# A hybrid encoder on one core: earlier tap loads, a moved gate block and moved table loads in the second mixer, a second buffer for blocks of b in the first

## The chip, the cores and the metric

The kernel runs on one core of a Trainium2 chip. The metric is the device time of one execution in microseconds (us); less is better. Several executions are timed and their median is given. Beside them stands one profiled execution, with a trace of every instruction on the five engines: PE (TensorE, matrix products; PEld are its weight loads), DVE (VectorE), ACT (ScalarE), POOL (GpSimd) and SP (SyncE, which only issues transfers here). ACT and POOL issue transfers as well.

## The reference

Two layers work on 256 tokens of 1024 features. Each has a mixer (a gated convolution beside a bidirectional state-space branch, "S5") and a feed-forward part, dense in layer 0 and with eight experts in layer 1. The change touches the mixers alone. Cut to what they compute:

```python
h = rms_norm(x, norm_mix_g[layer])
z = h @ w_in[layer]                       # 1024 -> 3584
conv_v, conv_g, ssm_u, gate_conv, gate_ssm = jnp.split(z, split_at, axis=-1)

# convolution branch: 512 channels, 31 taps, one filter per channel
c = conv_v * sigmoid(conv_g)
c = depthwise_conv(c, dw_w) + dw_b
br_conv = silu(layer_norm(c, ln_g, ln_b)) @ w_conv_proj

# S5 branch: 32 groups of 16 channels, 64 complex states, both directions
s[t] = a * s[t-1] + (q * b) @ u[t]        # a, q from a_re, a_im, log_dt
y[t] = Re(c @ s[t]) (both directions) + d * u[t]
y = gelu(y); y = y * sigmoid(y @ w_glu + b_glu)
br_ssm = y @ w_ssm_proj

x = x + (sigmoid(gate_conv) * br_conv + sigmoid(gate_ssm) * br_ssm) @ w_out
x = x + FFN(rms_norm(x, norm_ffn_g[layer]))   # dense, or top 2 of 8 experts
```

## The kernel before

Features lie on the 128 partitions and the 256 tokens along the free dimension. The program goes through the first mixer (to about 212 us), the dense feed-forward (to about 440 us), the second mixer (to about 660 us) and the experts.

**The mixer.** `z()` computes one block of 2 x 128 output columns of `w_in`, from two weight units of 512 KB each, into one PSUM tile `acc`. The blocks come in this order: two for the S5 input, four for the convolution's value and gate (`glu`), and eight gate blocks (`z_gate()`, numbered 0 to 7). Between blocks `step()` lets side work go on: the S5 scan (`sc_p`, `sc_q`, `eb`), the layer norm of the convolution (`conv_norm`), and what was put off (`later`). In layer 0 (`plain`) the weights go into PE as fp32 as they come. In layer 1 each unit is first split by ACT (`wh`) and DVE (`wl`), three units ahead at most.

**The convolution.** When half of the gated channels (`hc`) are ready, `shifted()` writes them to DRAM (one POOL transfer) and reads them back as eight shifted copies (`hs`, eight POOL transfers). `conv(h)` then does two tiles (`conv_tile`, 32 products each), and each tile needs one block of taps `dg` of 512 KB. The taps have two buffers. Each tile loads its own, on POOL's queue, behind the `hs` transfers of its half. The order in the mixer is: gate block 0, `conv(0)`, gate block 1, `conv(1)`, four more gate blocks, the S5 output for q = 0 and 1, gate block 6, q = 2 and 3, gate block 7.

**The S5 tables.** S5's output (`ssm_out`, four parts q) multiplies the states by tables `tq` and the input by a kernel `w` (w3), both made on the chip. Layer 0 makes its tables inside the mixer: DVE computes `tq`, and `build_g(q)` multiplies it on PE by a block of b (`bd`, 256 KB), and writes the result to DRAM (`gd`, half of it from POOL, half from ACT), from where w3 is read back by POOL. `bd` has one buffer, and POOL loads it:

```python
def load_bd(self, l, q):
    self.bd = self.bdp.tile([128, 8, 2, 2, 16], F32, name="bd")
    self.nc.gpsimd.dma_start(self.bd.rearrange("p g r h c -> p (g r h c)"), self.a["bd"][l, q])
```

Layer 1's tables are made during the dense feed-forward (`park`) and parked in DRAM (`dw`, `dt`, `gd`). In the second mixer `fetch` reads a parked `dt` back as `ft`, two of 512 KB for each q, through SP's queue, and POOL reads the four w3. These twelve tiles share eight buffers, in the order w3, ft, ft for each q, so the last four tiles take over buffers that the S5 output for q = 0 and 1 has read.

**Order of the work.** PE, DVE and ACT carry out their instructions in the order in which the program writes them. POOL and SP have their transfers placed by a scheduler, and then issue them in that order: a transfer that has to wait holds up all behind it on its engine.

Of the kernel before, what the change touches and what calls it, by code (L numbers as in the profile page):

```python
# [10 lines left out]
F32 = mybir.dt.float32  # L11
# [8 lines left out]
T = 256  # L20
# [38 lines left out]
class Body:  # L59
# [181 lines left out]
    def consts(self):  # L241
        nc, cp = self.nc, self.cp
        self.par = cp.tile([128, NPAR], F32, name="par")
        nc.scalar.dma_start(self.par, self.a["par"])
        self.x = cp.tile([128, 8, T], F32, name="x")
        self.xs = self.a["xt"].rearrange("(k p) t -> p k t", p=128)
        ji = self.smallp.tile([128, 128], I32, name="ji", bufs=1)
        nc.gpsimd.iota(ji, pattern=[[1, 128]], base=0, channel_multiplier=-1)
        self.ident = cp.tile([128, 128], F32, name="ident")
        nc.vector.tensor_scalar(self.ident, ji, 0, None, op0=ALU.is_equal)  # L250
        self.ones = cp.tile([128, 1], F32, name="ones")
        nc.vector.memset(self.ones, 1.0)

        self.bgh = cp.tile([128, 8], F32, name="bgh")
        n0, k0 = COLS["bglu", 0]
        nc.vector.tensor_scalar(self.bgh, self.par[:, n0:n0 + 8], 0.5, None, op0=ALU.mult)
# [196 lines left out]
        return t, self.table_steps(t, g0, cp[0][:, 0], cp[0][:, 1], pt, ALU.subtract)  # L453

    def load_bd(self, l, q):
        self.bd = self.bdp.tile([128, 8, 2, 2, 16], F32, name="bd")
        self.nc.gpsimd.dma_start(self.bd.rearrange("p g r h c -> p (g r h c)"), self.a["bd"][l, q])

    def build_g(self, l, b, cp, gd, q, tq):

        nc = self.nc
        cp, cm = cp
        bd = self.bd
        ps = self.misc()
        for s in range(2):
            for p in range(4):
                g = 4 * s + p
                for r in range(2):
                    self.mm(ps[32 * p:32 * p + 32, s * 128:(s + 1) * 128],
                            bd[:, g, r].rearrange("p h c -> p (h c)"), tq[s][:, p, r], r == 0, r == 1)  # L470
        for s in range(2):
            for p in range(4):
                g = 4 * s + p
                for r in range(2):
                    self.mm(ps[32 * p:32 * p + 16, 256 + s * 16:256 + (s + 1) * 16],
                            b[:, r, 8 * q + g], (cp[:, 0, 8 * q + g], cm[:, 8 * q + g])[r], r == 0, r == 1)
        gsb = self.t2("gsb", [128, 9, 2, 16])
        nc.scalar.copy(gsb[:, 1:9].rearrange("p m s c -> p s m c"),
                       ps[:, :256].rearrange("p (s m c) -> p s m c", s=2, m=8))
        for p in range(4):  # L480
            nc.scalar.copy(gsb[32 * p:32 * p + 16, 0].rearrange("p s c -> p (s c)"),
                           ps[32 * p:32 * p + 16, 256:288])
        for p in range(4):
            for eng, m0, n, r0, g0 in ((nc.gpsimd, 7, 8, 0, 0), (nc.scalar, 0, 7, 16, 2)):
                eng.dma_start(gd[m0:m0 + n, :, p].rearrange("m c s d -> c m (s d)"),
                              gsb[32 * p + r0:32 * p + r0 + 16, g0:g0 + n].rearrange("c m s d -> c m (s d)"))
# [171 lines left out]
    def mixer(self, l, fed=None, after=None):  # L658
# [39 lines left out]
                pass  # L698
        else:
            dw, dt, gd, a8 = self.parked  # L700
            hh, hl, sqs = fed
            w1s = []

# [64 lines left out]
        def ssm0_out():  # L768
            yield
            pt = self.ssm_prep_out(0)  # L770
            self.ssm_q()
            yield
            cps = []
            for _ in self.ssm_cq(0, c, cps):
                pass
            cp, gd_ = cps
            tqs = []
            for h in range(9):
                if h and h % 2 == 0:
                    q = h // 2 - 1  # L780
                    self.build_g(0, b, cp, gd_[q], q, tqs[2 * q:2 * q + 2])
                    ts.append((tqs[2 * q:2 * q + 2], self.load_w3(gd_[q])))
                if h < 8:
                    t, st = self.half_t(cp, pt, 4 * h)
                    tqs.append(t)
                    if h % 2 == 0:
                        self.load_bd(0, h // 2)
                    for _ in st:
                        pass
                    yield  # L790
            k = 1
            while k < 31:
                self.ssm_scan(eb, a8, k, min(k + 4, 31))
                k += 4
                yield
            ts.append(self.ssm_states(eb))
# [72 lines left out]
                step()  # L869

        z_gate()
        conv(0)
        z_gate()
        conv(1)
        if not plain:
            for q in range(4):
                w3 = self.load_w3(gd[q], self.last_dg)
                ts.append((self.fetch(dt[q]), w3))
        sides.append(self.conv_norm(l, cv))
        for i in range(5 if plain else 4):  # L880
            z_gate()
        while len(sides):
            step()
# [102 lines left out]

    def conv_tile(self, l, c, o, hs):

        dg = self.dgp.tile([128, 4, 8, 32], F32, name="dg")
        self.last_dg = ins = self.nc.gpsimd.dma_start(dg.rearrange("p i m c -> p (i m c)"), self.a["cdg"][l, c])  # L990
        self.behind(ins.ins, self.last_hs[c // 2].ins)
        for m in range(8):
            for i in range(4):
                self.mm(o[32 * i:32 * i + 32], dg[:, i, m], hs[:, i, 4 * m:4 * m + T], m == 0, m == 7)

    def conv_bias(self, l, h, ps, cv):
        dwb = self.col("dwb", l)
# [78 lines left out]
        self.nc.gpsimd.dma_start(d, t.rearrange("p g r m -> p (g r m)"))  # L1076
        return d

    def fetch(self, ds):
        out = []  # L1080
        for d in ds:
            t = self.tb("ft", [128, 4, 2, 128])
            ins = self.nc.sync.dma_start(t.rearrange("p g r m -> p (g r m)"), d)
            self.behind(ins.ins, self.last_raw.ins)
            out.append(t)
        return out

# [73 lines left out]
    def route_feed(self):  # L1161
# [15 lines left out]
        def after(i):  # L1177
# [9 lines left out]
                products(i - 1)  # L1187
            if i == 3:
                products(3)
                self.lt = self.rp.tile([8, T], F32, name="lt")  # L1190
                nc.scalar.copy(self.lt, st[0][0:8, :T])
                self.rs = self.rms_of(st[1][:, :2])
        return after
# [530 lines left out]
    def moe_consts(self):  # L1724
# [1 line left out]
        self.iota = cp.tile([128, 128], F32, name="iota")  # L1726
        nc.gpsimd.iota(self.iota, pattern=[[1, 128]], base=0, channel_multiplier=0,
                       allow_small_or_imprecise_dtypes=True)
        io = self.smallp.tile([128, 128], I32, name="ji", bufs=1)
        nc.gpsimd.iota(io, pattern=[[1, 128]], base=0, channel_multiplier=-1)  # L1730
        self.before = cp.tile([128, 128], F32, name="before")
        nc.vector.tensor_scalar(self.before, io, 0, None, op0=ALU.is_gt)
# [109 lines left out]
    def pool(self, ctx, name, bufs, **kw):  # L1842
        if kw.get("space") != DRAM:
            kw["reuse_waits"] = "tile"
        return ctx.enter_context(self.tc.tile_pool(name=name, bufs=bufs, **kw))
# [10 lines left out]
    def run(self):  # L1856
        pool = self.pool
        with ExitStack() as ctx:
# [12 lines left out]
            with self.ordered():  # L1871
                with ExitStack() as c2:
# [2 lines left out]
                    self.setp2 = pool(c2, "set2", 1)  # L1875
                    self.hcp = pool(c2, "hc", 1)
                    self.h4p = pool(c2, "h4", 5)
                    self.bdp = pool(c2, "bd", 1)
                    self.later, self.sides, self.firsts, self.last_hs = [], [], [], [None, None]
                    self.t2p = pool(c2, "t2", 2)  # L1880
                    self.dgp = pool(c2, "dg", 2)
# [111 lines left out]
```

## Time and profile before

| | us |
|---|---|
| median of 3 runs | 1397.8 (1396.7 to 1401.72) |
| profiled execution, its own time | 1396.65 |
| span of its trace | 1394.8 |
| PE busy in the span | 1310.5 (94%) |
| DVE, ACT, POOL busy | 870.5, 622.3, 84.4 |

A span is the time from the first to the last instruction of the trace; what lies around it makes the 1.85 us between it and that execution's own time. Times in rows are us from the start of the span, unless they are marked ns. The trace gives the start, the duration and the tiles of every instruction, the idle time ahead of it, and what that idle time ended with ("<-"); "issue" stands there where the profile shows no releaser. The granted clock of PE is a share of full speed: 1.00 is 2.4 GHz and 0.50 is 1.2 GHz.

### The profile page before, as it was taken

Reading aid. Unit: us, or ns where it says so; the run is one execution under the profiler, and the core shown is the slowest. Engines: PE = TensorE matmul, PEld = TensorE weight load, DVE = VectorE, ACT = ScalarE, POOL = GpSimd, SP = SyncE. Lnnn points to the kernel's source line nnn. Section 1 sums busy time; section 2 is a strip of 40 time slices with the busy share of each in tenths; the row PEclk is TensorE's granted clock in tenths of the full one; section 3 lists DMA queues with packets and bytes.
Section 4 is the critical chain, followed back from the end, with each engine's and each line's share of the span. In section 5 each row is a group of like instructions: output and inputs, shape, how many; then the busy total and the mean of one; then the engine's idle time right before and its main releaser. Section 6 shows DMA issues by size and latency. Waiting matters only on the chain.

```text
span 1394.8 us, 23390 instructions
## 1 busy us (share of the span) xinstructions
PE 1310.5 (94%) x9324; PEld 1032.6 (74%) x9324; DVE 870.5 (62%) x1332; ACT 622.3 (45%) x905; POOL 84.4 (6%) x148
## 2 busy tenths in 40 slices
PE   7999989999998978989899999999999999999995
PEld 6877889999998967878766666666666666666663
DVE  7696676788887455774755555545555555565552
ACT  3432345444444442543445544445444545454542
POOL 1052130000121031000000000000000000000000
PEclk9999999999999999999799999999999999999996
DMA  6285535566778475544589999999999999999980
GB/s 223 87 258 163 165 126 168 174 215 209 224 236 297 143 259 173 197 137 167 204 330 421 409 421 358 364 411 420 418 398 367 421 421 420 420 401 421 421 362 32
DMA packets 78306, 399.73 MB, mean 287 GB/s; under 512 B 13024, under 2 KB 15712, under 8 KB 44400
## 3 DMA queue, kind: packets, MB, share of 16 engines
q1 hardware_dynamic: 64960, 370.70, 69.1%
q0 software_dynamic: 8448, 26.32, 5.9%
q10 hardware_dynamic: 4784, 1.16, 0.4%
q8 instruction: 75, 1.23, 0.4%
q14 instruction: 39, 0.32, 0.1%
HBM read 386.51 MB, written 11.63 MB: 285 GB/s over the span
## 4 chain that ended last, share of the span: by engine, by line
PE 59%; DVE 5%; DMA 3%; ACT 2%; issue 1%; ACTq 0%; SPq 0%; DVEq 0%; POOLq 0%
PE acc L122 36%; PE py L122 9%; PE pys L122 6%; PE misc L122 4%; PE misc L130 2%; DVE wl L75 2%; PE mix L122 1%; ACT wh L93 1%; DMA ft<-dt 1%; DMA hc<-hc 1%; DMA hs<-hc 0%; DMA dg<-in_cdg 0%; PE dn L122 0%; DVE yl L87 0%; ACT yh L1577 0%
## 5 line engine op out<-in xcount | busy, mean ns | idle before, releaser
L75 DVE TENSOR_TENSOR wl<-raw,wh 128x1024 fp32r<-128x1024 f32 x394 | 473.9, 1222 | 236.8 <-ACT wh L93 236.7
L93 ACT ACTIVATE wh<-raw 128x1024 fp32r<-128x1024 f32 x394 | 408.0, 1055 | 78.2 <-PE acc L122 34.9
L122 PE MATMUL acc<-wh,x 128*128 128x512 f32 x704 | 232.8, 400 | 0.0
L122 PE MATMUL acc<-raw,xs 128*64 128x256 f32 x1408 | 171.9, 387 | 0.0
L122 PEld LDWEIGHTS acc<-wh,x 128*128 128x128 f32 x704 | 132.6, 188 | 32.2 <-issue 1.0
L122 PE MATMUL acc<-wl,x 128*128 128x512 f32 x352 | 138.4, 393 | 5.9 <-DVE wl L75 5.9
L122 PEld LDWEIGHTS acc<-raw,xs 128*64 128x64 f32 x1408 | 95.9, 137 | 61.8 <-issue 21.5
L122 PE MATMUL acc<-hf,wh 128*128 128x256 f32 x704 | 126.8, 283 | 0.0
L122 PE MATMUL acc<-xg,raw 128*128 128x256 f32 x448 | 106.0, 395 | 6.6 <-DMA raw<-in_w_in 6.6
L122 PE MATMUL acc<-hh,wh 128*128 128x256 f32 x352 | 104.5, 297 | 6.9 <-ACT hh L642 3.1
L122 PEld LDWEIGHTS acc<-hf,wh 128*128 128x128 f32 x704 | 107.7, 188 | 0.2
L122 PE MATMUL acc<-hh,wl 128*128 128x256 f32 x352 | 102.6, 291 | 1.7 <-DVE wl L75 1.7
L122 PE MATMUL acc<-hl,wh 128*128 128x256 f32 x352 | 102.5, 291 | 0.1
L122 PEld LDWEIGHTS acc<-xg,raw 128*128 128x128 f32 x448 | 87.8, 199 | 19.8 <-ACT xg L688 6.5
L122 PE MATMUL acc<-hf,wl 128*128 128x256 f32 x352 | 99.0, 281 | 1.4 <-DVE wl L75 1.4
L122 PE MATMUL pys<-raw,mas 128*64 128x512 f32 x352 | 85.2, 605 | 0.4 <-ACT mas L1509 0.4
L122 PEld LDWEIGHTS acc<-wl,x 128*128 128x128 f32 x352 | 66.7, 189 | 19.8 <-DVE wl L75 6.8
L1500 ACT ACTIVATE sl<-acc,gs 128x256 f32<-128x256 f32 x44 | 20.9, 475 | 130.9 <-PE acc L122 130.9
L87 DVE SCALAR_TENSOR_TENSOR sl<-acc,gs,sl 128x256 f32<-128x256 f32 x44 | 21.2, 483 | 91.4 <-ACT sl L1500 91.4
L122 PEld LDWEIGHTS acc<-hh,wh 128*128 128x128 f32 x352 | 70.3, 200 | 10.7 <-issue 4.0
L122 PE MATMUL py<-wh,mah 128*128 128x512 f32 x176 | 73.3, 417 | 0.0
L122 PEld LDWEIGHTS acc<-hh,wl 128*128 128x128 f32 x352 | 70.3, 200 | 2.3 <-DVE wl L75 2.3
(308 smaller groups left out, 1967.2 us busy)
## 6 DMA issues: line engine op xcount, KB each, us to landing
raw<-in_m_gu SPq DMA_DIRECT2D x176, 1024.0 KB, 8.8
raw<-in_m_down SPq DMA_DIRECT2D x88, 1024.0 KB, 9.1
raw<-in_w_in SPq DMA_DIRECT2D x56, 512.0 KB, 4.1
raw<-in_f_gate SPq DMA_DIRECT2D x22, 512.0 KB, 3.5
raw<-in_f_up SPq DMA_DIRECT2D x22, 512.0 KB, 3.8
raw<-in_f_down SPq DMA_DIRECT2D x22, 512.0 KB, 3.7
raw<-in_w_out SPq DMA_DIRECT2D x16, 512.0 KB, 3.6
hs<-hc POOLq DMA_DIRECT2D x32, 142.0 KB, 5.5
```

What stands on the lines that cost most here:

```text
L75: return self.nc.vector.tensor_tensor(out, a, b, op=op)
L87: return self.nc.vector.scalar_tensor_tensor(out, a, s, b, op0=op0, op1=op1)
L93: self.nc.scalar.activation(h, raw, AF.Copy)
L122: return self.nc.tensor.matmul(out, l, r, start=start, stop=stop, **kw)
L130: return self.nc.tensor.transpose(out, in_, self.ident)
L1500: nc.scalar.activation(sl, pg[:, :n], AF.Silu, scale=gs[:, 1:2])
```

## The change

In the first mixer `bd` gets two buffers, and for layer 0 ACT issues its loads instead of POOL: the first two before the first table is used, the third and the fourth after `build_g(0)` and `build_g(1)`. In the second mixer the first two blocks of taps are asked for at the mixer's start, gate block 1 goes ahead of `conv(0)` (so two gate blocks stand before it, one between the two halves and three behind), and the parked tables `ft` are read through POOL's queue, behind the last taps, instead of SP's. Three small tiles (`ji` twice, `lt`) move to another pool, which makes the room for the second `bd` buffer.

```diff
     def load_bd(self, l, q):
-        self.bd = self.bdp.tile([128, 8, 2, 2, 16], F32, name="bd")
-        self.nc.gpsimd.dma_start(self.bd.rearrange("p g r h c -> p (g r h c)"), self.a["bd"][l, q])
+        bd = self.bdp.tile([128, 8, 2, 2, 16], F32, name="bd")
+        eng = self.nc.gpsimd if l else self.nc.scalar
+        eng.dma_start(bd.rearrange("p g r h c -> p (g r h c)"), self.a["bd"][l, q])
+        self.bds[l, q] = bd
...
             dw, dt, gd, a8 = self.parked
+            for c in range(2):
+                self.dgs[l, c] = self.load_dg(l, c)
...
                     if h % 2 == 0:
-                        self.load_bd(0, h // 2)
+                        for q in range(h // 2, min(h // 2 + 2, 4)):
+                            if (0, q) not in self.bds:
+                                self.load_bd(0, q)
...
         z_gate()
+        if not plain:
+            z_gate()
         conv(0)
         z_gate()
         conv(1)
         if not plain:
             for q in range(4):
                 w3 = self.load_w3(gd[q], self.last_dg)
-                ts.append((self.fetch(dt[q]), w3))
+                ts.append((self.fetch(dt[q], self.last_dg), w3))
         sides.append(self.conv_norm(l, cv))
-        for i in range(5 if plain else 4):
+        for i in range(5 if plain else 3):
             z_gate()
...
     def conv_tile(self, l, c, o, hs):
 
-        dg = self.dgp.tile([128, 4, 8, 32], F32, name="dg")
-        self.last_dg = ins = self.nc.gpsimd.dma_start(dg.rearrange("p i m c -> p (i m c)"), self.a["cdg"][l, c])
-        self.behind(ins.ins, self.last_hs[c // 2].ins)
+        if (l, c) in self.dgs:
+            dg = self.dgs.pop((l, c))
+        else:
+            dg = self.load_dg(l, c)
+            self.behind(self.last_dg.ins, self.last_hs[c // 2].ins)
...
-    def fetch(self, ds):
+    def fetch(self, ds, after=None):
...
-            ins = self.nc.sync.dma_start(t.rearrange("p g r m -> p (g r m)"), d)
-            self.behind(ins.ins, self.last_raw.ins)
+            eng = self.nc.sync if after is None else self.nc.gpsimd
+            ins = eng.dma_start(t.rearrange("p g r m -> p (g r m)"), d)
+            self.behind(ins.ins, (after or self.last_raw).ins)
...
-                    self.bdp = pool(c2, "bd", 1)
+                    self.bdp = pool(c2, "bd", 2)
```

On POOL, in the second mixer, this stood before: the write of the first half of `hc`, its eight `hs`, the two `dg` of `conv(0)`, the second half's `hc` and `hs`, its two `dg`, and the w3 loads (`w<-gd`).

```order
L979 DMA hc_0_5353<-hc 128x2x288
L984 DMA hs<-hc_0_5353 32x4x284 x8
L990 DMA dg<-in_cdg 128x1024 x2
L979 DMA hc_1_5553<-hc 128x2x288
L984 DMA hs<-hc_1_5553 32x4x284 x8
L990 DMA dg<-in_cdg 128x1024 x2
L492 DMA w<-gd_0_3677 128x8x128
L492 DMA w<-gd_1_3678 128x8x128
```

At the same place there stands now:

```order
L987 DMA hc_0_5357<-hc 128x2x288
L992 DMA hs<-hc_0_5357 32x4x284 x8
L987 DMA hc_1_5557<-hc 128x2x288
L992 DMA hs<-hc_1_5557 32x4x284 x8
L1008 DMA dg<-in_cdg 128x1024 x2
L494 DMA w<-gd_0_3677 128x8x128
L1099 DMA ft<-dt_0_3962 128x1024
L1099 DMA ft<-dt_1_3964 128x1024
L494 DMA w<-gd_1_3678 128x8x128
```

The first two `dg` have left this place (POOL issues them in the first mixer now, once the last use of their buffers there is over), and the parked tables `ft<-dt` stand between the w3 loads.

On SP, the weight units of the second mixer (`raw`) and the parked tables stood in this order before, from the eighth unit on:

```order
L111 DMA raw<-in_w_in 128x1024 x15
L1083 DMA ft<-dt_0_3962 128x1024
L1083 DMA ft<-dt_1_3964 128x1024
L1083 DMA ft<-dt_0_4215 128x1024
L1083 DMA ft<-dt_1_4217 128x1024
L1083 DMA ft<-dt_0_4468 128x1024
L111 DMA raw<-in_w_in 128x1024 x6
L111 DMA raw<-in_w_cproj 128x1024 x2
L111 DMA raw<-in_w_glu 128x1024
L1083 DMA ft<-dt_1_4470 128x1024
L111 DMA raw<-in_w_glu 128x1024
L1083 DMA ft<-dt_0_4721 128x1024
```

Now the weights stand alone:

```order
L111 DMA raw<-in_w_in 128x1024 x21
L111 DMA raw<-in_w_cproj 128x1024 x2
L111 DMA raw<-in_w_glu 128x1024 x2
L111 DMA raw<-in_w_cproj 128x1024 x2
L111 DMA raw<-in_w_sproj 128x1024 x4
```

No weight unit stands behind a parked table any more.

On ACT, in the first mixer, these are the rows around the first `build_g` now (`cm` is one of its inputs, `eb` are the S5 sums, `gsb` its result, `gd` the write of that result):

```order
L447 ACTIVATE cm<-cp 128x512
L458 DMA bd<-in_bd 128x512 x2
L534 COPY eb<-mix 64x2x8x32
L535 COPY eb<-mix 64x2x8x32
L845 ACTIVATE gt<-gt 128x512
L480 COPY gsb<-misc 128x2x8x16
L483 COPY gsb<-misc 16x32 x4
L487 DMA gd_0_670<-gsb 16x7x32 x4
L458 DMA bd<-in_bd 128x512
L731 ACTIVATE gate<-gate 128x512
```

The two rows `bd<-in_bd` are new there; before, POOL issued the blocks among its `hs`, `dg` and `gd` transfers.

## Rows read from the trace of the kernel before

**Rows 1.** Stretches: us, busy of PE, PEld, DVE, ACT, POOL, PEclk, DMA, GB/s
```profile
101.60:107.50 5.90, 0.02 (x2) 0.05 (x3) 5.83 (x7) 0.00 (x0) 0.00 (x0) 0.94 0.81 310
...
512.00:516.00 4.00, 2.87 (x28) 1.61 (x32) 1.56 (x9) 0.00 (x0) 0.00 (x0) 0.50 1.03 412
...
532.00:536.00 4.00, 4.00 (x43) 1.79 (x38) 0.63 (x4) 0.00 (x0) 0.00 (x0) 0.50 1.02 325
```

**Rows 2.** Waits of PE, 440 to 670 us: us in total, times, longest
```profile
PE mix L122 <- issue: 7.2, 1, 7.2
...
PE mix L122 <- DMA dg<-in_cdg: 3.1, 1, 3.1
PE mix L122 <- DMA ft<-dt: 1.9, 2, 1.5
```

**Rows 3.** Waits of PE, 0 to 200 us
```profile
PE misc L122 <- DMA bd<-in_bd: 5.9, 1, 5.9
```

**Rows 4.** Timeline of PE, first mixer: start, us, tiles, [idle before <- releaser]
```profile
86.16 7.11 PE L122 MATMUL mix<-hs,dg 128*32 128x256 f32 x128
...
107.48 1.96 PE L122 MATMUL misc<-tq,bd 128*32 128x128 f32 x32 [5.92 <-DMA bd<-in_bd]
...
109.59 7.39 PE L122 MATMUL mix<-hs,dg 128*32 128x256 f32 x128
116.80 1.11 PE L122 MATMUL misc<-tq,bd 128*32 128x128 f32 x32
```

**Rows 5.** Timeline of PE, second mixer
```profile
513.13 8.70 PE L122 MATMUL mix<-hs,dg 128*32 128x256 f32 x128 [7.22 <-issue]
...
530.86 10.06 PE L122 MATMUL mix<-hs,dg 128*32 128x256 f32 x128 [3.09 <-DMA dg<-in_cdg]
...
580.93 0.64 PE L122 MATMUL mix<-ft,s 128*32 128x128 f32 x16 [1.52 <-DMA ft<-dt]
```

**Rows 6.** Chain of waits, second mixer: start, us, what
```profile
508.92 8.14 DMA hc<-hc
...
517.67 6.44 DMA hs<-hc
...
524.70 6.12 DMA dg<-in_cdg
```

**Rows 7.** Timeline of POOL, second mixer (issues of transfers)
```profile
501.07 3.81 POOL L984 DMA_DIRECT2D hs<-hc  x7 [2.15 <-issue]
504.88 1.11 POOL L990 DMA_DIRECT2D dg<-in_cdg  x2
...
570.82 0.88 POOL L492 DMA_DIRECT2D w<-gd  x1 [42.01 <-PE mix L122]
```

**Rows 8.** Timelines of POOL and of ACT, first mixer
```profile
97.25 0.56 POOL L990 DMA_DIRECT2D dg<-in_cdg  x1
97.80 0.55 POOL L457 DMA_DIRECT2D bd<-in_bd  x1
...
87.77 2.30 ACTq L485 DMA_DIRECT2D gd<-gsb  x2
```

**Rows 9.** Timeline of DVE, both mixers
```profile
99.25 1.22 DVE L75 TENSOR_TENSOR tq<-tq,tmp 128x1024 f32<-128x1024 f32 x1
...
565.35 2.07 DVE L552 COPY s<-eb 64x992 f32<-64x992 f32 x2
```

**Rows 10.** Transfers issued in 97.2:97.5, 494:500, 500:505, 526:530: KB, us to landing
```profile
dg<-in_cdg POOLq DMA_DIRECT2D x1, 512.0 KB, 8.8
...
hc<-hc POOLq DMA_DIRECT2D x1, 288.0 KB, 3.6
...
hs<-hc POOLq DMA_DIRECT2D x7, 142.0 KB, 5.8
...
w<-gd POOLq DMA_DIRECT2D x3, 512.0 KB, 10.2
...
raw<-in_w_in SPq DMA_DIRECT2D x1, 512.0 KB, 8.8
```

More of the change, by code (lines that the diff above doesn't have):

```diff
@@ L246, in consts @@
         self.xs = self.a["xt"].rearrange("(k p) t -> p k t", p=128)
-        ji = self.smallp.tile([128, 128], I32, name="ji", bufs=1)
+        ji = self.c2("ji", [128, 128], I32)
         nc.gpsimd.iota(ji, pattern=[[1, 128]], base=0, channel_multiplier=-1)
@@ L462, in build_g @@
         cp, cm = cp
-        bd = self.bd
+        bd = self.bds.pop((l, q))
         ps = self.misc()
@@ L994, in conv_tile, with load_dg @@
                 self.mm(o[32 * i:32 * i + 32], dg[:, i, m], hs[:, i, 4 * m:4 * m + T], m == 0, m == 7)
+    def load_dg(self, l, c):
+        dg = self.dgp.tile([128, 4, 8, 32], F32, name="dg")
+        self.last_dg = self.nc.gpsimd.dma_start(dg.rearrange("p i m c -> p (i m c)"), self.a["cdg"][l, c])
+        return dg
     def conv_bias(self, l, h, ps, cv):
@@ L1189, in after @@
                 products(3)
-                self.lt = self.rp.tile([8, T], F32, name="lt")
+                self.lt = self.c2("lt", [8, T])
                 nc.scalar.copy(self.lt, st[0][0:8, :T])
@@ L1728, in moe_consts @@
                        allow_small_or_imprecise_dtypes=True)
-        io = self.smallp.tile([128, 128], I32, name="ji", bufs=1)
+        io = self.c2("ji", [128, 128], I32)
         nc.gpsimd.iota(io, pattern=[[1, 128]], base=0, channel_multiplier=-1)
@@ L1877, in run @@
                     self.h4p = pool(c2, "h4", 5)
-                    self.bdp = pool(c2, "bd", 1)
+                    self.bdp = pool(c2, "bd", 2)
+                    self.dgs, self.bds = {}, {}
                     self.later, self.sides, self.firsts, self.last_hs = [], [], [], [None, None]
```

## The prediction

> **What bounds the kernel now.** I read the waits of PE first, then the timeline of PE around each long wait, then the chain of waits and POOL's timeline to see what the wait hung on. PE is busy for 94% of the span, so only time in which PE stands still, or runs at its lower clock, can be won. Of the waits that this change touches there are four. In the first mixer PE waits 5.92 us for a block of b [rows 3, 4]. In the second it waits 7.22 us ahead of `conv(0)` and 3.09 us ahead of `conv(1)` [rows 2, 5], and 1.9 us for parked tables [rows 2]. After each of the two waits at the convolution the granted clock is 0.50, the lower of PE's two levels [rows 1]: the same convolution half takes 8.70 and 10.06 us there [rows 5] and 7.11 us in the first mixer, where PE came to it without a pause [rows 4].
>
> **The first mixer.** The third block of b left POOL at 97.80, behind a tap load of 97.25 [rows 8], and PE could use it at 107.48 [rows 4]: 9.7 us. PE had come to it at 107.48 - 5.92 = 101.56. With two buffers ACT issues this block right behind its `gd` writes, the last of which ended at 87.77 + 2.30 = 90.07 [rows 8]. Even with the same 9.7 us it is there at 99.8, so the wait of 5.92 goes. What is late next: the sixth table `tq`, which the same products need, is ready at 99.25 + 1.22 = 100.47 [rows 9], 1.1 us before PE. Then comes `conv(1)`; its second taps were issued at 97.25 [rows 8] and take 8.8 us [rows 10], so they land at 106.05. PE comes to them after the table products (1.11), the small ones behind them (109.59 - 107.48 - 1.96 = 0.15) and half of 7.11, at 106.4. That is just in time. After the wait PE was slow: the 32 table products took 1.96 us there and 1.11 later, the convolution 7.39 instead of 7.11 [rows 4]. So this part is worth 5.92 + 0.85 + 0.28 = 7.05 us, at least about 5 if taps or table are 2 us late.
>
> The loads of b now stand in ACT's order: two ahead of the copies of the S5 sums, one each behind the first two `gd` writes. Two `gd` writes with their waits held ACT for 2.30 us [rows 8]; four loads at half of that each are 4.6 us, in a stretch where ACT waits for PE (it is idle all through 101.60 to 107.50 [rows 1]). I take 0, with 2.3 as the other end.
>
> **The second mixer, up to conv(1).** PE came to `conv(0)` at 513.13 - 7.22 = 505.91. The row names no releaser, but the two taps were issued last, from 504.88 to 505.99 behind the `hs` [rows 7], and with 7 to 8 us to landing they are what PE waited for. They are now loaded long before, in the first mixer. One gate block takes 530.86 - 3.09 - 513.13 - 8.70 = 5.94 us. With one more ahead PE comes to `conv(0)` at 511.85. The last `hs` of this half was issued at about 504.3 (seven in 3.81 us from 501.07 [rows 7]) and lands 5.8 later [rows 10], at 510.1. So nothing is left of the 7.22 (margin 1.7). `conv(0)` at 7.11 ends at 518.96, the next gate block at 524.9.
>
> Then `conv(1)` needs its own `hs` and taps. Before, this was a chain: the write of `hc` at 508.92 took 8.14, the first `hs` 6.44, the taps 6.12, and they landed at 530.8 [rows 6]. Beside the write ran two tap loads and five parked tables, and the transfers were full (share 1.03 [rows 1]); all seven are gone from this stretch. The first half's write took 3.6 [rows 10]. I take 4.6 for the second, near that end: `hs` from about 514.1, eight issues of 0.54 to 518.5, taps behind them, landing at 524.6 with 6.12. The second taps need the buffer of `conv(0)`'s second tile, free at 519, and land at 525 to 526 with 6.12; PE wants them at 524.9 + 3.6 = 528.5. With 8.14 for the write instead everything is 3.5 later and PE waits about 3.2; with taps at 8.8, up to 6. I take 0.7, bounds 0 and 6. This part is worth 7.22 + 3.09 + (8.70 - 7.11) + (10.06 - 7.11) - 0.7 = 14.15 us.
>
> **The parked tables.** Five of them went out early on SP; now POOL issues all eight, between the w3 loads, behind the last taps, from about 519.6. Eight of the twelve tiles (three w3, five `ft`) have free buffers at once: 8 x 0.52 MB = 4.2 MB. POOL's queue moved two taps and three w3 (2.6 MB) from 524.70 [rows 6] to about 528.8 + 10.2 = 539 [rows 10], 183 GB/s beside the weights. At that rate the eight are there at 542.6. PE needs them when the S5 output begins; its first part was over when POOL's last w3 could go, at 570.82 [rows 7], which is about 555 now. That is 12 us of cover, and 0 it costs. The last four tiles wait for that first part in both kernels, and PE waited 1.9 for them [rows 2]. Now they stand in one queue: four issues of 0.55 to 0.88 us, 2.1 MB, 11.5 us at 183 GB/s, against one gate block and one part of S5 output (5.94 + 2.7) and the 1.9 of before. So PE would wait 2.9 instead of 1.9. Bounds are a gain of 1.9 and a loss of 5; I take a loss of 0.5, near the row of before, since the tables no longer stand behind weight units on SP.
>
> The Trainium skill, page SBUF — State Buffer, section SBUF: two separate sides, speaks against this move: a transfer issued from GpSimd needs GpSimd to write its descriptors, and a VectorE copy in fp32 between SBUF tiles locks it out for as long as it runs. Such a copy here is `s<-eb`, 2.07 us for the two [rows 9]. By that rule the sum would be up to 2.1 us smaller if a table's issue fell beside it; by the order it falls between the first eight issues (over by about 527) and the last four (after the first part of S5 output), and no run so far shows the two together.
>
> **The sum.** 7.05 + 14.15 - 0.5 = 20.7 us. The profiled execution's own time is 1396.65 (span 1394.8 and 1.85 around it), so 1375.95 for it. The median is 1.15 above that execution: 1397.8 - 20.7 = **1377.1 us**. The experts behind it start their transfers as soon as the second mixer's buffers are free, so they move as one and give nothing back. An edit of 0.5%, 7 us, is about what a measurement of this kernel can tell from no change.
>
> **The rivals.**
> *POOL stays the chain's last link* (chance 0.15). The first wait goes, but hc, hs and taps of the second half stay as slow as in [rows 6], because the weights alone fill the transfers. `conv(1)` then starts at 530.86 as before, 6 us after PE comes, and at the low clock (10.06). For it: POOL's issues are serial, and a unit of weights took up to 8.8 us [rows 10]. Against it: 3.6 us for the first half's write. Gain 20.7 + 0.7 - 6 - 2.95 = 12.5: 1385.
> *The gain is given back at the S5 output* (0.10). Only three gate blocks stand behind `conv(1)` now, and the last four tables come through POOL. If these land 5 us late and the eight 5 us after PE's arrival, the gain is 10: 1388. For it: PE already waits there [rows 5]; against it: the 12 us of cover.
> *No change* (0.07). The moved gate block uses up DVE's and ACT's lead: DVE is busy 5.83 of 5.90 us while PE waits in the first mixer [rows 1], so DVE would be the next bound and the same time shows as waits for `wl`, `tq` or `s`. Gain 0 to 6: about 1394. Against it: the sixth table is ready 1.1 us before PE would need it.
> *Slower* (0.06). POOL's queue is starved. Two taps and twelve tiles are behind one another on it, 6.3 MB of tiles from 519.6, and PE wants the last at about 565. At 139 GB/s they are in time; below about 93 GB/s (68 us) the loss passes the 21.9 us won from the waits, and at 85 GB/s the kernel is 7 us slower: 1405. For it: the tiles of w3 are in short pieces and took 10.2 us [rows 10]. Against it: the 183 GB/s above.
>
> **How the numbers follow.** The forecast has 0.62; its own range is 1373 (the 1.9 us gone too, POOL's 0.7 and the 0.5 not lost) to 1381. The range that should hold 8 in 10 takes in the first two rivals in part: 1372 to 1389. Faster by over 0.5% (below 1390.8): 0.62 + 0.15 + most of 0.10, that is 0.85. Within 0.5%: 0.09. Slower: 0.06.
>
> **What would show it.** In the changed profile there should be no wait of PE for `bd`; PE should go from gate block 1 into `conv(0)` without idle time, both halves at some 7.1 us, at a granted clock near 1.00; `conv(1)` should wait less than 1 us; the second mixer's S5 output should begin some 21 us earlier in the span. I am wrong if `conv(1)` still waits several us for `hs` or `dg`, or if waits for `ft`, `w`, `wl` or `s` grow by more than a few us.

## The result and the profile after

The changed kernel takes 1383.09 us (median of 4 runs, 1378.31 to 1383.94) against 1397.55 (median of 4, 1396.7 to 1401.72): a ratio of 0.9887, 95% interval 0.986 to 0.9914. The forecast was 1377.1 us, the range 1372 to 1389. The profiled execution has a span of 1380.5 us against 1394.8, at a mean granted clock of 0.975 against 0.969.

The timeline of PE in the first mixer and then in the second: start, us, what, and in brackets the idle time before with its releaser. The third block's products and the halves of the convolution answer to [rows 4, 5].

```profile
83.59 1.12 PE L122 MATMUL misc<-tq,bd 128*32 128x128 f32 x32 [0.98 <-DMA bd<-in_bd]
...
85.61 7.11 PE L122 MATMUL mix<-hs,dg 128*32 128x256 f32 x128 [0.61 <-DMA dg<-in_cdg]
...
100.94 1.12 PE L122 MATMUL misc<-tq,bd 128*32 128x128 f32 x32
...
102.36 7.11 PE L122 MATMUL mix<-hs,dg 128*32 128x256 f32 x128
...
506.59 7.11 PE L122 MATMUL mix<-hs,dg 128*32 128x256 f32 x128
...
519.90 7.11 PE L122 MATMUL mix<-hs,dg 128*32 128x256 f32 x128 [0.25 <-DMA dg<-in_cdg]
...
561.71 0.64 PE L122 MATMUL mix<-ft,s 128*32 128x128 f32 x16 [1.96 <-DMA ft<-dt]
562.17 0.40 PE L122 MATMUL mix<-w,up 128*32 128x128 f32 x8
564.22 1.08 PE L122 MATMUL mix<-ft,s 128*32 128x128 f32 x16 [1.66 <-DMA ft<-dt]
```

The three waits that the change was to reach are gone: the third block of b has no idle time ahead of it (5.92 before), `conv(0)` none (7.22), `conv(1)` 0.25 (3.09), and every half of the convolution takes 7.11. Two waits are new, for the first block (0.98) and for the first taps (0.61) of the first mixer; there was neither in the kernel before. The waits for the parked tables grew from 1.9 to 3.62 us, and the last row shows what they leave behind: 16 products in 1.08 us instead of 0.64.

The transfers on POOL around it, from its timeline (an issue's start and length, and the wait before it), which answer to [rows 6, 7]:

```profile
503.89 0.72 POOL L987 DMA_DIRECT2D hc<-hc  x1 [4.27 <-DVE sc_q L75]
508.13 4.37 POOL L992 DMA_DIRECT2D hs<-hc  x8 [3.52 <-issue]
512.49 0.57 POOL L1008 DMA_DIRECT2D dg<-in_cdg  x1
...
550.49 0.53 POOL L1099 DMA_DIRECT2D ft<-dt  x1 [28.24 <-PE mix L122]
551.15 0.91 POOL L494 DMA_DIRECT2D w<-gd  x1
552.04 1.06 POOL L1099 DMA_DIRECT2D ft<-dt  x2
```

The `hs` start 4.24 us after the write of `hc` is issued (8.75 before, [rows 6]); the write itself takes 3.7 us to land (8.14 before). The chain of waits has the first taps of `conv(1)` and the last of these tables as links:

```profile
512.49 7.37 DMA dg<-in_cdg
...
552.57 11.61 DMA ft<-dt
```

From the first issue at 550.49 to the last landing at 564.18 are 13.7 us for four tiles. The stretches (us, busy time of PE, PEld, DVE, ACT and POOL with counts, granted clock, DMA share, GB/s) show the clock: at the two places of [rows 1] in the second mixer it is 1.00 now, behind the tables it is 0.50, and once more low at 596.

```profile
512.00:516.00 4.00, 4.00 (x51) 3.15 (x44) 2.62 (x14) 1.89 (x4) 2.59 (x5) 1.00 1.05 256
532.00:536.00 4.00, 4.00 (x29) 3.79 (x29) 3.30 (x11) 0.49 (x1) 0.00 (x0) 1.00 1.02 378
...
564.00:570.00 6.00, 5.78 (x44) 5.33 (x45) 2.88 (x4) 0.00 (x0) 0.00 (x0) 0.50 0.12 29
596.00:600.00 4.00, 2.95 (x13) 2.75 (x14) 2.43 (x3) 1.58 (x2) 0.00 (x0) 0.67 0.48 135
```

**Where the gain comes and goes.** The same instruction is looked up in both traces, and its start in the changed kernel is taken from its start before: that is the lead at this place. The places are DVE's first `u` (27.04 us before), its `hc` behind the first mixer's convolution (127.07), `u` of the second mixer (466.21), PE's first product of the second mixer's S5 output (569.19) and DVE's first `m` behind it (615.18). The last column of leads compares the ends of the two spans. The table has every kernel of the study (its edits are told below); each row is one profiled execution, the ratio is from the timed runs. f1 is e2 and f2 is b1 once more, the same code.

| kernel | 27 | 127 | 466 | S5 output | 615 | end | ratio, 95% interval |
|---|---|---|---|---|---|---|---|
| the change | 1.6 | 7.5 | 5.2 | 19.7 | 13.9 | 14.3 | 0.9887 (0.986 to 0.9914) |
| a1 first mixer only | -0.6 | 3.9 | 2.4 | 1.9 | 1.8 | 2.7 | 0.995 (0.9931 to 0.9969) |
| a2 taps and gate block only | 0.9 | 0.7 | -1.9 | 2.9 | 3.7 | 4.6 | 0.9962 (0.9941 to 0.9983) |
| a3 tables on SP | -0.3 | 4.1 | 2.6 | 8.5 | 9.3 | 10.5 | 0.9904 (0.9873 to 0.9935) |
| a4 first block on POOL | -0.6 | 2.2 | -1.2 | 12.8 | 10.0 | 8.5 | one run |
| d1 no gate block ahead | 1.4 | 5.1 | 3.8 | 9.6 | 3.2 | 4.3 | 0.9968 (0.9955 to 0.9981) |
| d2 no early taps | -0.8 | 3.4 | 1.8 | 14.5 | 11.3 | 11.9 | 0.9893 (0.9875 to 0.9912) |
| e1 two gate blocks | -0.5 | 4.5 | 2.9 | 14.5* | 12.5 | 13.0 | 0.9874 (0.9841 to 0.9907) |
| b1 spare buffers | 1.3 | 3.6 | 0.8 | 15.8 | 18.1 | 22.2 | 0.9812 (0.9793 to 0.9832) |
| c1 b1, blocks and taps early | -0.5 | 6.5 | 5.9 | 20.7 | 23.0 | 24.2 | 0.9812 (0.9789 to 0.9835) |
| e2 b1, blocks early | 0.0 | 7.1 | 6.7 | 21.5 | 23.8 | 27.9 | 0.9816 (0.977 to 0.9863) |
| f1 e2 once more | 1.4 | 6.3 | 3.3 | 18.2 | 20.6 | 22.7 | 0.9826 (0.9789 to 0.9863) |
| f2 b1 once more | -0.5 | 5.0 | 2.8 | 17.0 | 19.3 | 24.4 | 0.9833 (0.9806 to 0.986) |

(* 20.4 less the gate block of 5.94 that it has not run yet.)

For the change: 1.6 at the start, 5.9 in the first mixer, -2.3 up to the second, 14.5 in its convolution, -5.8 behind it, and 0.8 up to the last norm (14.75; the spans differ by 14.3). The first, the third and the last of these terms were not in the forecast.

### The profile page after: what moved, and what is told of

The parts are those of the page before. It is cut to its first block, busy times and chain, and to the rows that moved or that the text cites. A ratio compares the mean times of both kernels' runs of the same rounds, so it can differ in the third digit from the quotient of the medians.

```text
span 1380.5 us, 23395 instructions
## 1 busy us (share of the span) xinstructions
PE 1304.0 (94%) x9324; PEld 1030.2 (75%) x9324; DVE 870.6 (63%) x1332; ACT 621.9 (45%) x905; POOL 86.3 (6%) x152
## 4 chain that ended last, share of the span: by engine, by line
PE 61%; DVE 5%; DMA 2%; ACT 1%; issue 1%; POOL 0%; ACTq 0%; DVEq 0%
PE acc L122 38%; PE py L122 9%; PE pys L122 6%; PE misc L122 4%; PE misc L130 2%; PE mix L122 1%; DVE wl L75 1%; DMA ft<-dt 1%; DMA dg<-in_cdg 1%; ACT wh L93 1%; PE dn L122 0%; DVE yl L87 0%; ACT yh L1593 0%; DVE x L75 0%; POOL hs L992 0%
## 5 line engine op out<-in xcount | busy, mean ns | idle before, releaser
L122 PEld LDWEIGHTS acc<-raw,xs 128*64 128x64 f32 x1408 | 95.9, 137 | 61.8 <-issue 21.5
L122 PEld LDWEIGHTS acc<-xg,raw 128*128 128x128 f32 x448 | 86.2, 196 | 19.3 <-ACT xg L690 6.5
```

The costliest lines, as they stand in the source:

```text
L122: return self.nc.tensor.matmul(out, l, r, start=start, stop=stop, **kw)
```

## The experiments

**Which part gives what: a1, a2, a3.** a1 is the kernel before with one edit, the blocks of b in two buffers and on ACT. a2 is the kernel before with the taps and the gate block alone, tables on SP. a3 is the change with one line undone:

```diff
-                ts.append((self.fetch(dt[q], self.last_dg), w3))
+                ts.append((self.fetch(dt[q]), w3))
```

a1, expected: 

> The kernel before with the first mixer's part alone: blocks of b in two buffers, loaded by ACT (lt and ji moved as in the change). Theory (each part's gain stands by itself): the second mixer stays as before (conv(0) waits about 7.2 us, conv(1) about 3.1 us), the S5 output of the first mixer starts about 7.5 us earlier than before (1.6 of it already at the first gate block, since the 256 KB block no longer shares the DMA engines with the first weights; 5.9 from the wait for the third block; about 1.1 of clock; less about 1.6 of new waits for the first block and the first taps), and the time is 1390 us (ratio 0.9947). Rival (an earlier first mixer lowers the clock later: in the changed kernel 2.3 of 7.5 us were lost at 452 to 460 us, at a granted clock of 0.60 against 0.79): the lead shrinks to about 5.2 us at the start of the second mixer, and the time is 1392.4 us (0.9963). Second rival (the 1.6 us at the start were chance): lead 5.9 at the S5 output.

a2, expected: 

> The kernel before with the second mixer's taps loaded early and the gate block moved ahead of the conv; the parked tables stay on SP and the first mixer stays as before. Theory (the tables on SP start beside the hc write, which took 8.14 us before and 4.2 us in the changed kernel where the tables were behind the taps): conv(0) has no wait, conv(1) waits 2 to 6 us, middle 4.4, because hc lands 3.9 us later than in the changed kernel; the last four tables cost 1.9 us as before and the clock stays at 1.00 behind them; lead at the start of the S5 output about 14.5 - 4.4 = 10 us, and of it nothing is lost behind it: 1387.5 us (0.9927). Rival (the order of gate and conv does it all, the queue of the tables is no matter): conv(1) waits below 1 us, lead 14.5 us, time 1383 us (0.9896). Second rival (an earlier S5 output finds its last tables late on any queue): ft waits of about 3.6 us and the clock at 0.5 to 0.8 behind them, 1389 us or more.

a3, expected: 

> The changed kernel with the parked tables back on SP. Theory: hc lands 3.9 us later, conv(1) waits 2 to 6 us (middle 4.4) instead of 0.25; the waits for the last four tables are about 1.9 us instead of 3.6 and the clock stays at 1.00 behind them, which returns about 5.8 us: both about cancel, 1382 us (0.989), range 1379 to 1386. Rival (the queue is no matter for the taps): conv(1) below 1 us, 1377.5 us (0.9856). Second rival (an earlier S5 output finds the last tables late on any queue): both losses stand, 1387 us (0.9925).

Measured: 1392.6, 1391.74 and 1387.45 us, each slower than its theory. In a1 the lead behind the first mixer is 3.9 us instead of 7.5: the 1.6 us at the start are not there (-0.6; the second rival had that right), and the mixer itself gives 3.9 + 0.6 = 4.5 instead of the change's 5.9, since its taps are waited for 2.5 us, longer than in the change. Its time is the first rival's, but of the lead only 1.6 us go between the mixers. In a2 and a3 `conv(1)` waits longer than the theory's 6 us. The timeline of PE in a3:

```profile
509.05 7.11 PE L122 MATMUL mix<-hs,dg 128*32 128x256 f32 x128
...
528.37 9.84 PE L122 MATMUL mix<-hs,dg 128*32 128x256 f32 x128 [6.26 <-DMA dg<-in_cdg]
```

Of a3's transfers issued from 515 to 517 us (out<-in, queue, count, KB each, us to landing), the taps and one table:

```profile
dg<-in_cdg POOLq DMA_DIRECT2D x2, 512.0 KB, 13.9
ft<-dt SPq DMA_DIRECT2D x1, 512.0 KB, 17.6
```

With the tables on SP the taps take 13.9 us instead of the change's 7.4, and `conv(1)` waits 6.26 us (7.30 in a2) and runs at the low clock again. So the tables on SP cost about as much as the forecast's theory said, but by another link: the `hs` followed the write of `hc` almost as soon as in the change (issue at 506.36, `hs` at 510.86, 4.50 us), and it was the taps that the tables slowed. The Trainium skill, page DMA: Bandwidth & Descriptors, section Queues, rings and completion order, says that each transfer engine takes turns between the queues that have work; the trace agrees with that: the first of these taps, issued at 515.21, was there after 13.1 us, before the table that SP had issued at 514.91 (17.6 us). But a3 changes the tables' time with their queue: SP issued the five from 512.25 on, ahead of the taps, where in the change they are issued behind them. No run has them on SP and behind the taps, so how much of the 6 us is the queue and how much the order is not shown. In a2 and a3 PE waits 1.1 us for the last tables, and no lead is lost behind the S5 output (+0.8 in both): both rivals fall.

**The gate block and the early taps: d1, d2.** Each undoes one of the two in the change.

```diff
         z_gate()
-        if not plain:
-            z_gate()
         conv(0)
...
-        for i in range(5 if plain else 3):
+        for i in range(5 if plain else 4):
```

```diff
-            for c in range(2):
-                self.dgs[l, c] = self.load_dg(l, c)
```

d1, expected: 

> The changed kernel without the gate block that was moved ahead of conv(0) of the second mixer (four blocks stand behind conv(1) again); taps and tables as in the change. Theory (the shifted reads of the second half, not the taps, set when conv(1) can start, so that the gate block fills a wait that is there anyway): conv(0) waits about 3 us for the first half's shifted reads, conv(1) about 3 us for its taps behind the second half's, conv(1) starts where it did (about 520 us of the span), and the S5 output about 6 us later; time 1389 us (0.9938). Rival (the early taps and the freed queue are enough, the gate block is no matter): both waits below 1 us, time 1383 us (0.9896).

d2, expected: 

> The changed kernel without the early loads of the second mixer's first two tap tiles (they are issued behind the first half's shifted reads again); gate block and tables as in the change. Theory (1 MB of taps then stands in POOL's queue just ahead of the second hc write): conv(0) waits about 1 us (0 to 2.5), hc lands 2 to 4 us later than in the changed kernel and conv(1) waits as much; time 1387 us (0.9925). Rival (the gate block covers the taps, loading them early gives nothing more): both waits below 1 us, time 1383 us. Second rival (the taps were what bounded it): conv(0) waits 5 us or more, 1390 us.

Measured: d1 1392.27 us, slower than the theory's 1389; d2 1383.92, the rival's time, with waits nearer the theory's. The timeline of PE in d1:

```profile
502.03 7.25 PE L122 MATMUL mix<-hs,dg 128*32 128x256 f32 x128
...
522.17 9.19 PE L122 MATMUL mix<-hs,dg 128*32 128x256 f32 x128 [6.94 <-DMA dg<-in_cdg]
```

The same in d2:

```profile
510.24 7.11 PE L122 MATMUL mix<-hs,dg 128*32 128x256 f32 x128 [0.37 <-DMA dg<-in_cdg]
...
525.11 7.11 PE L122 MATMUL mix<-hs,dg 128*32 128x256 f32 x128 [1.82 <-DMA dg<-in_cdg]
```

The timeline of POOL in d2, at the second half's write:

```profile
507.09 0.72 POOL L985 DMA_DIRECT2D hc<-hc  x1 [3.35 <-DVE sc_q L75]
514.77 4.38 POOL L990 DMA_DIRECT2D hs<-hc  x8 [6.96 <-PE mix L122]
```

Without the gate block the whole wait stands at `conv(1)`, 6.94 us; `conv(0)` has none, against the 3 expected there. In d2 the write of `hc` is 3.4 us slower with 1 MB of taps in the queue ahead (7.1 us to its landing at 514.2, against 3.7; the row of the `hs` names a product of PE, which was over just before, at 513.9). That is as expected, but only 2.2 us of it reach PE. The three edits don't add: from 466 us to the S5 output a2 and a3 (no tables on POOL) gain 4.8 and 5.9 us, d1 (no gate block) 5.7, d2 (no early taps) 12.6, all three 14.5. The gate block and the new place of the tables each need the other, since either alone leaves 6.3 to 7.3 us of wait at `conv(1)`.

**The late tables: b1 and e1.** b1 keeps the change and puts three of the last four tiles into buffers that are free by then: two of the taps' pool, one of the pool of the shifted reads and gates.

```diff
+            dgt = lambda name, shape: self.dgp.tile(shape, F32, name=name, tag="dg")
+            gtt = lambda name, shape: self.gtp.tile(shape, F32, name=name, tag="gate")
             for q in range(4):
-                w3 = self.load_w3(gd[q], self.last_dg)
-                ts.append((self.fetch(dt[q], self.last_dg), w3))
+                w3 = self.load_w3(gd[q], self.last_dg, dgt if q == 3 else self.tb)
+                tiles = {2: (self.tb, dgt), 3: (gtt, self.tb)}.get(q, (self.tb, self.tb))
+                ts.append((self.fetch(dt[q], self.last_dg, tiles), w3))
```

Expected: 

> The changed kernel with three of the last four tables in buffers that are free by then (two of the taps' and one of the shifted convs' buffers), so that eleven of the twelve are loaded by about 535 us and one alone waits for the first S5 output block. Theory (the late tables and the lower clock that their waits leave cost 5.8 us): waits for ft go from 3.6 us to at most 0.7, the granted clock is 1.00 from 549 to 614 us of the span, and the time is 1377.5 us (ratio 0.9856). Rival (the lower clock comes from what the engine does there at any rate, not from the waits): the waits go, clock still 0.5 to 0.8 near 564 and 597 us, and the time is 1381 us (0.988). Second rival (three more transfers of 512 KB beside the weights of the gate blocks delay those): a wait for wh or raw of 2 to 5 us appears between 520 and 550 us, time 1383 us or more.

Measured: 1372.93 us, below the theory's 1377.5. The timeline of PE in the last two S5 blocks of b1:

```profile
562.13 0.64 PE L122 MATMUL mix<-ft,s 128*32 128x128 f32 x16
...
562.81 0.62 PE L122 MATMUL mix<-ft,s 128*32 128x128 f32 x16
...
563.46 0.62 PE L122 MATMUL mix<-ft,s 128*32 128x128 f32 x16
...
564.12 0.62 PE L122 MATMUL mix<-ft,s 128*32 128x128 f32 x16
```

The stretches of b1 from the start of the S5 output on:

```profile
553.40:565.00 11.60, 11.60 (x242) 11.05 (x242) 7.53 (x11) 4.93 (x6) 0.54 (x1) 1.00 0.69 228
565.00:579.00 14.00, 12.46 (x101) 12.14 (x102) 11.61 (x17) 6.91 (x11) 0.00 (x0) 1.00 0.36 114
579.00:610.00 31.00, 25.74 (x199) 24.07 (x198) 22.14 (x27) 14.14 (x20) 0.00 (x0) 1.00 0.44 136
```

No wait for a table, and no low clock up to 610. (Behind that it falls to 0.50 for some 3 us, at the same products as in the kernel before, there from 628 to 632.) The lead rises by 2.3 between the S5 output and 615, where the change loses 5.8: the late tables cost 8.1 us, more than expected because the 1.9 of the kernel before went too. The lead rises by the same 2.3 or 2.4 in c1, e2, f1 and f2, which all have these buffers. Behind 615 the trace of b1 wins another 4.0 us that no edit accounts for, nearly all of it at the very end: the products that ran from 1359 to 1363 and from 1377 to 1381 before, at a granted clock of 0.59 and 0.50, ran at 1.00 and 0.95. From 615 to the end e2 and f2 win 4.1 and 5.1, c1 and f1 1.2 and 2.1; the cause stays open.

e1 covers them instead: two gate blocks between the second and the third S5 block, one fewer ahead.

```diff
-        for i in range(5 if plain else 3):
+        for i in range(5 if plain else 2):
...
             if q == 2 and not plain:
                 z_gate()
+                z_gate()
```

Expected: 

> The changed kernel with two gate blocks instead of one between the second and the third S5 output block of the second mixer (one fewer stands ahead of the first); buffers and queues of the change. Theory (the last four tables are late because one gate block of 5.95 us stands between their buffers' release and their use; the scan's states are ready at 546.5 us of the span, so the first S5 output block, which could start at 543.6, waits about 3 us for them): the waits for ft are below 0.5 us, a wait of 2 to 4 us for s takes their place, the clock behind the tables is 1.00, time 1380 us (ratio 0.9875). Rival (the lower clock comes back behind the wait for s as it did behind the one for ft): 1383 us (0.989). Second rival (the tables land late whatever covers them): ft waits above 2 us, 1386 us.

Measured: 1381.96 us, between theory and first rival, and not to be told from the change's 1383.09 (the intervals overlap). The longest of PE's waits from 540 to 600 us in e1 (us in total, times, longest):

```profile
PE mix L122 <- DVE s L554: 2.0, 2, 1.9
...
```

Two stretches of e1 behind that wait:

```profile
548.00:554.00 6.00, 5.06 (x92) 4.66 (x96) 4.49 (x7) 3.69 (x7) 2.48 (x4) 0.52 0.56 185
554.00:558.00 4.00, 4.00 (x39) 3.62 (x32) 2.30 (x3) 0.21 (x1) 0.00 (x0) 0.87 0.88 298
```

The tables are in time, but the scan's states `s` are not, and the low clock follows that wait as it followed the other. In e1 the cover only moved the wait; with more buffers, in b1, it went.

**The first mixer's new waits: a4, c1, e2.** a4 gives the first block of b back to POOL (`eng = self.nc.gpsimd if l or q == 0 else self.nc.scalar`). c1 and e2 stand on b1 and issue the first two blocks on ACT while the S5 sums begin; c1 has the first two tap tiles with them (the last two lines below), e2 has not:

```diff
                     for i in range(2):
                         self.ssm_turn(u, up, i)
+                    for j in range(2):
+                        self.load_bd(0, j)
+                    for j in range(2):
+                        self.dgs[l, j] = self.load_dg(l, j, nc.scalar)
```

a4, expected: 

> The changed kernel with the first mixer's first block of b issued by POOL again (at about 1.5 us, as before the change); the other three by ACT. Theory (the 1.6 us ahead at the first gate block was the clock granted at the start, not the block's 256 KB): the first gate block ends within 1 us of where it does in the kernels with all blocks on ACT; the wait for the first block (1.0) is gone and the one for dg is no longer than in them (0.6 to 2.5). Rival (the block beside the first weights costs 1.6 us): the first gate block ends 1 to 2 us later, as before the change.

c1, expected: 

> b1_spare_buffers with, in the first mixer, the first two blocks of b and the taps of the first two conv tiles issued by ACT some 20 us earlier (behind the up copies, at about 54 us, instead of 76 us). Theory (the blocks moved off the start meet the shifted reads and the taps at 76 to 88 us, and that is where the new waits of 1.04 for bd and 2.52 for dg in b1 come from): both waits are gone, the clock stays at 1.00 through the first conv, and the time is 3 to 5 us below b1, 1369.5 us (ratio 0.979). Rival (the DMA engines are as full at 54 us, with the weights of the gate blocks): a wait for raw of 1 to 3 us between 54 and 76 us takes the place, time 1373 us (0.9812). Second rival (behind the first waits the next taps are late, since nothing is loaded faster): conv(1) of the first mixer waits 2 to 3 us for dg, 1372.5 us.

e2, expected: 

> c1_first_loads_early with the first mixer's two blocks of b issued early (at about 54 us) and its taps where the change has them (behind the shifted reads, at about 77 us). Theory (512 KB of blocks beside the taps delay the taps): the wait for bd is gone and the one for dg falls from 2.5 us in b1_spare_buffers to about 1; time 1371.5 us (ratio 0.981). Rival (the taps are late by their own place in the queue): the wait for dg rises to about 3.5 us, since conv(0) is reached 1 us earlier, and the time is that of b1.

Measured: a4 1388.19 (one run), c1 1372.34, e2 1368.99 us. In c1 both waits went, as its theory had it, and neither rival's wait came, but its time is that of b1 (1372.93). ACT issued the loads from 46.4 us in e2, earlier than the 54 of the expectations. The taps and blocks of the change, among its transfers issued from 75.8 to 78 us:

```profile
dg<-in_cdg POOLq DMA_DIRECT2D x2, 512.0 KB, 10.4
bd<-in_bd ACTq DMA_DIRECT2D x2, 256.0 KB, 8.8
```

The taps of e2, issued from 77.6 to 79 us:

```profile
dg<-in_cdg POOLq DMA_DIRECT2D x2, 512.0 KB, 8.2
```

The timeline of PE in e2:

```profile
84.19 0.66 PE L122 MATMUL misc<-tq,bd 128*32 128x128 f32 x16
85.12 0.67 PE L122 MATMUL misc<-tq,bd 128*32 128x128 f32 x16 [0.28 <-DVE tq L75]
...
86.07 7.11 PE L122 MATMUL mix<-hs,dg 128*32 128x256 f32 x128
```

With the 512 KB of blocks out of the way the taps land in 8.2 us instead of 10.4, and both waits are gone without any tap being issued sooner; in a4, with 256 KB still there, the taps took 10.7 and the wait for them was 2.55. The other kernels say the same: two taps take 6.5 to 8.9 us where no block is loaded beside them (before, a2, e2, f1) and 10.4 to 11.8 where one or two are (the change and eight more). So it was the blocks that made the taps late, more than e2's theory had it. From 27 to 127 us c1 and e2 gain 7.0 and 7.1; the eight kernels with the first mixer of the change gain 2.3 (b1) to 5.9 (the change). The block at the start is not what cost 1.6 us there: with it a4 has -0.6 and a2 0.9, and of the kernels without it six have -0.8 to 0.0 and three 1.3 to 1.6.

Whether this lead is in the time was asked once more, with both side by side:

f1, expected: 

> e2_blocks_early once more, in five rounds, side by side with b1_spare_buffers. Theory (the first mixer's lead of 4.8 us over b1 that the trace of e2 shows at 127 us less the different starts, 7.1 - 2.3, stands in the time): 1368.5 us, 4 to 5 us (0.003 of the ratio) below b1. Rival (the clock takes it back behind, as it seemed in c1): the same time as b1 within 1.5 us.

f2, expected: 

> b1_spare_buffers once more, on the chip of f1_blocks_early_again: 1373 us (ratio 0.982) by either theory.

Measured: 1371.69 us (0.9826, 0.9789 to 0.9863) and 1375.03 (0.9833, 0.9806 to 0.986). The medians differ by 3.3 us in the theory's direction, but the intervals overlap and the profiled executions stand the other way round (spans 1372.1 and 1370.4). In f1 the two waits are gone again, with taps that land in 6.5 us, but another has come, for the second taps of the first mixer's `conv(1)`, which took 11.2:

```profile
107.07 3.66 PE L122 MATMUL mix<-hs,dg 128*32 128x256 f32 x64 [1.94 <-DMA dg<-in_cdg]
```

That is the second rival of c1, which neither c1 nor e2 showed, and from 27 to 127 us f1 gains 4.9 and f2 5.5. So it is shown, in three kernels, that blocks loaded early take the two waits away; it is not shown that this gains time. That the spare buffers beat the changed kernel is shown: the interval of b1 (0.9793 to 0.9832) ends below the change's (from 0.986), and that of f2 ends at it (0.986).

## Why the prediction was right, and where it was off

**Second mixer up to conv(1): right.** 14.15 us forecast, 19.7 - 5.2 = 14.5 measured; 14.0 to 15.0 in a4, b1, c1 and e2, which have this part whole. `conv(0)` without idle time, `conv(1)` 0.25 for 0.7, 7.11 for both halves, 3.7 for 4.6 for the write of `hc`. One reason was too broad: the prediction put the 8.14 us of `hc` to two taps and five tables beside it. d2 shows that the taps alone slow the write to 7.1. In a3 the tables were issued only at 512.25, behind that write, and what they slowed was the taps; what they would do beside `hc` no run shows apart.

**First mixer: the mechanism right, the size short.** The 5.92 went, and with it the low clock (1.12 for 1.96, 7.11 for 7.39); the sixth table and the second taps were in time, as worked out. The step that failed is "I take 0, with 2.3 as the other end" for ACT's loads. It asked what they cost ACT, not what their 512 KB cost the taps: waits of 0.98 + 0.61 = 1.6 us in the change, 3.6 in b1. The forecast's 7.05 came out only where the blocks were loaded early (7.0 and 7.1), and there not each time: f1 gains 4.9, since it waits 1.94 us for the second taps, which the prediction had "just in time".

**The parked tables: the step that failed.** "I take a loss of 0.5", bounds -1.9 to 5; it was 5.8. The eight early ones were in time, as said. The last four took 13.7 us, not 11.5, and PE waited 3.62, not 2.9. The larger part was not in the sum at all: 5.8 less the 1.7 of longer waits are 4.1 us, for which the trace shows the lower of PE's two levels from 564 to 570 and again near 597. The lead goes from 19.7 to 18.0 in the waits, to 15.4 in the first of these stretches and to 13.9 in the second. That the second hangs on the tables is shown only in so far as none of the five kernels with b1's buffers has either; a4 has the second alone. In part this is the rival that gives the gain back at the S5 output.

The low clock is not certain behind such a wait. It came behind 3.6 us for `ft` in the change, 4.1 in d1 and 3.7 in d2, but a4, with 3.7, lost only 2.8 us and stood at 1.00 for 30 us behind it. Behind 1.1 to 2.0 us for `ft` (before, a1, a2, a3) it did not come. In e1 it came behind 2.0 us for `s`, but PE had stood 1.24 us for `rl` just before (from 545.3 to 548.8 us it was busy for 0.4). In the first mixer, behind 2.5 us for the taps, `conv(0)` took 8.80 in b1 and a4 and 7.11 in a1. The Trainium skill, page TensorE: Matmul & The Clock Gate, section HAM oscillation — how this bites in real kernels, says that a wait for transfers can bring PE back to half rate each time; the traces agree for three of the four kernels that wait 3.6 us and more for `ft`.

**What the forecast left out.** "They move as one and give nothing back" holds for the experts in the change, but not for the stretch between the mixers: the lead falls by 2.3 there, at a granted clock of 0.60 in a stretch that had 0.79 before. First before, then the change:

```profile
460.00:468.00 8.00, 8.00 (x57) 8.00 (x57) 4.61 (x15) 1.33 (x2) 0.00 (x0) 0.79 0.45 131
```

```profile
452.50:460.50 8.00, 8.00 (x45) 8.00 (x46) 3.19 (x14) 0.00 (x0) 0.00 (x0) 0.60 0.42 127
```

Every kernel of the table loses between 127 and 466 us, 0.4 to 3.3 us, a2 too, which changes nothing ahead of it but the time of two tap loads (at 116.6): in that stretch the one execution of before was among the quick ones. At the start it is the other way round (1.6 won). Against the forecast's 20.7 the start, the first mixer and the stretch behind it make 1.6 - 1.1 - 2.3 = -1.8 us, the late tables -5.3, the second mixer and the end +0.3 + 0.8: the 6 us by which the gain was short. A slip of the prediction beside this: the terms that it names for the lower end of its own range give 1374.0, not 1373.

The Trainium skill's rule on GpSimd's descriptors, which the prediction weighed, was not put to the test: `s<-eb` ran at 544.5 to 546.5, and POOL issued nothing between 522.3 and 550.5.

## What to carry over

When a transfer is moved to another time or queue, price what it does to the transfers that are under way there and will be waited for, not only what it costs the engine that issues it. Tables that wait for buffers are helped by a buffer that happens to be free, less by more work ahead of their use. And a single profiled execution has its own clock: where nothing was changed the lead fell by 0.4 to 3.3 us from 127 to 466 us, and from 615 to the end it moved by anything from -1.5 (a4) to 5.1 (f2). A lead is compared place by place and over several kernels before an edit is credited with it.

## What was not expected of the hardware

- The granted clock differs between executions at places where nothing was changed: 0.91 in the change and 0.77 in c1 from 20 to 40 us (PE busy for 15.30 and 17.28 us there); 0.66 in c1 behind the second mixer, at 677 to 687 us, where b1 had 1.00. The same code taken twice differs too: at 27 us b1 and f2 lead by 1.3 and -0.5, e2 and f1 by 0.0 and 1.4.
- The same 512 KB of taps took 7.4 us with the tables behind them in the queue, 13.9 with the tables on another queue and issued from 3 us before them on, and 10.4 beside two blocks of 256 KB on ACT's.
- In none of the fourteen kernels (107 to 116 transfers on POOL in each) did POOL issue a transfer before the one eight places ahead of it in its order had landed. Behind the taps of `conv(1)` in the change, the idle times below end 0.3 us after that landing; the issue at 516.98, for one, follows an `hs` that landed at 516.70. Whether the chip or the program asks for this no run shows.

```profile
515.02 0.91 POOL L494 DMA_DIRECT2D w<-gd  x1 [0.43 <-DMA hs<-hc]
516.98 0.53 POOL L1099 DMA_DIRECT2D ft<-dt  x1 [0.52 <-DMA hs<-hc]
520.14 0.90 POOL L494 DMA_DIRECT2D w<-gd  x1 [0.54 <-DMA dg<-in_cdg]
```
